# Ordering early output products around a LayerNorm's sums, and holding GpSimd's additions until the keys are written

## The chip, the cores and the metric

The kernel runs on one core of a Trainium2 chip. Five engines work side by side, each through its own queue in order: TensorE (PE in the profile; its weight loads are PEld), VectorE (DVE), ScalarE (ACT), GpSimd (POOL), and SyncE (SP), which only starts transfers. TensorE reads on-chip memory (SBUF) and writes accumulation banks (PSUM); each tile of 128x512 float32 fills one bank. The metric is the device time of one execution in microseconds (us). A difference of less than 0.2% is hardly told from none here.

## The reference

Two layers of an encoder over 512 tokens of width 1024. Each layer has a SwiGLU block, then a mixing block, then another SwiGLU block and a norm. The change lies in the mixing block, of which this is the core (names as in the reference, with what does not matter left out):

```python
p = h @ w_in[l]
attn = mla_group(p[..., :o_kv], ...)      # 8 heads, queries and keys normalised per head
conv = conv_group(p[..., o_cv:], conv_w[l], conv_b[l], conv_ln_g[l], conv_ln_b[l])
x = x + jnp.concatenate([attn, conv], axis=-1) @ w_out[l]

def conv_group(u_raw, conv_w, conv_b, ln_g, ln_b):
    a, g = u_raw[..., :CONV_W], u_raw[..., CONV_W:]
    u = a * jax.nn.sigmoid(g)
    y = causal depthwise convolution of u, 31 taps
    return jax.nn.silu(layer_norm(y + conv_b, ln_g, ln_b))
```

In `mla_group` the keys are `k = rms_norm(k, k_g)` per head, and attention is chunk-causal with a softmax. So the output projection has eight blocks of 128 rows as its input: four from attention, four from the convolution. The four from attention do not depend on the convolution's LayerNorm.

## The kernel before

**Products.** Every float32 product is made of three matmuls (`mm3`, L166 to L168) on operands that were split into a high part and a remainder: high by high, high by remainder, remainder by high. ScalarE makes the high part (`A.copy`, L173 in `split`), VectorE the remainder (L174).

**Who sets the order.** The program is written as if for one queue. A scheduler with a model of time then places the instructions of each engine; an instruction that is placed later in its engine's queue waits for all ahead of it. `tc.issue_after(ins)` forbids the scheduler to place an instruction of the same engine ahead of `ins`; it adds no wait between engines. `tc.high_priority(CHAIN)` lets the scheduler prefer the instructions inside.

**The keys.** `keys()` makes, for each of four token blocks `t`, the keys' scale `sck` on GpSimd (a power, `rsqrt`, L185) and writes the normalised keys `kn` with two VectorE operations (L816 for 64 columns per head, L818 for 32). `turn(h)` transposes them on TensorE (L849). `order["keys"]` is the last of the four `rsqrt` operations. GpSimd's convolution additions (L970) for taps from `PAUSE` = 16 on, or for channel block 2, and the four transfers that GpSimd starts for the output weights (L154), are kept behind `order["keys"]`.

**The convolution.** Of four blocks of 128 channels, VectorE does blocks 0 and 3 tap by tap (L964), ScalarE and GpSimd do block 1 (ScalarE the product `pr`, L968, in four buffers; GpSimd the addition, L970), and TensorE does the early taps of block 2 (L672) with the rest of its taps on ScalarE and GpSimd. These are spread through the attention of the eight heads: scores (L868), maxima on VectorE (L872), exponentials on ScalarE (L876), transposed probabilities (L891), values (L913), division on VectorE (L916).

**The LayerNorm.** The four blocks are summed (`ysum`, L988 to L990), TensorE makes the mean (`pm`, L992), VectorE subtracts it (L994), ScalarE squares (L196, L199) and VectorE adds the squares (L203). Then one chain runs from engine to engine: TensorE sums over channels (`Stats.sums`, L210, four small matmuls), VectorE adds the epsilon (L217), GpSimd takes the power (L185), VectorE lays the result out as a diagonal (L225), TensorE spreads it over all channels (`spread`, L229), VectorE multiplies (L1006), ScalarE applies gain, bias and silu (L1008), and `split` makes the operands of the convolution's four blocks.

**The early products.** While that chain runs, TensorE can do the attention half of the first four output blocks (`WOG` = 4 banks, 48 matmuls). `early_groups` writes them bank by bank, four attention blocks each: the first bank (`E1` = 1) ahead of the chain, three banks behind it in the program, all behind the last score matmul of head 7. Then follow the convolution's 48 matmuls of these banks, and the other four output blocks.

```python
        early_groups(range(E1))
        ...
            r = st.token(CW, conv_bank)
            pr = spread(r, conv_bank, u[1])
        ...
        early_groups(range(E1, WOG))
```

Of the kernel before, what the change touches and what calls it, by code (L numbers as in the profile page):

```python
# [12 lines left out]
ALU = mybir.AluOpType  # L13
# [6 lines left out]
KD = D // P  # L20
NT = S // P
H = 8
DN = 64
DR = 32
DQ = DN + DR
# [25 lines left out]
GLUP = 0  # L51
EARLY = "s"
PRELOAD = 1
E1 = 1
WOG = 4
CHAIN = 400
WAKE = 10
# [20 lines left out]
def encoder_kernel(ctx: ExitStack, tc: tile.TileContext, xT, consts, vecs, rgain, wgu1, wd1, wdq1,  # L78
# [11 lines left out]
    def nm(s):  # L90
        uid[0] += 1
        return f"{s}{uid[0]}"
# [7 lines left out]
    def bank():  # L100
        return psum.tile([P, S], FP, tag="ps", name=nm("ps"))
# [10 lines left out]
    def tiny(tag, w, dt=FP):  # L112
        return small.tile([P, w], dt, tag=tag, name=nm(tag))

    V, A, G, T = nc.vector, nc.scalar, nc.gpsimd, nc.tensor
# [15 lines left out]
    minus_half = cpool.tile([P, H], FP, name="minus_half")  # L131
# [29 lines left out]
        return wpool.tile([P, WC], FR, tag="wl", name=nm("wl"))  # L161

    order = {}

    def mm3(o, lh, ll, rh, rl, first, last, free=False):
        T.matmul(o, lh, rh, start=first, stop=False, skip_group_check=free)  # L166
        T.matmul(o, lh, rl, start=False, stop=False, skip_group_check=free)  # L167
        order["mm"] = T.matmul(o, ll, rh, start=False, stop=last, skip_group_check=free).ins  # L168
        return order["mm"]
# [52 lines left out]
    def spread(r, made=bank, dg=None):  # L222

        dg = tmp() if dg is None else dg
        V.tensor_tensor(dg.rearrange("p (t j) -> p t j", t=NT),  # L225
                        ident[:, None, :].to_broadcast([P, NT, P]),
                        r[:, :, None].to_broadcast([P, NT, P]), ALU.mult)
        ps = made()
        order["spread"] = T.matmul(ps, ones, dg, start=True, stop=True).ins  # L229
        return ps  # L230
# [7 lines left out]
    def group(o, w, rhs, ks, n, ts=slice(0, S)):  # L238

        for k in ks:  # L240
            c = slice(k * P, (k + 1) * P)
            order["product"] = mm3(o, w[0][:, c], w[1][:, c], rhs[k][0][:, ts], rhs[k][1][:, ts], k == 0, k == n - 1)
# [386 lines left out]
    def mix_body(kpool, l, gx, norm, done):  # L629
        u, order = [], {}  # L630
# [53 lines left out]
        kn = kpool.tile([P, NT, H, DQ], FP, tag="kn", name=nm("kn"), bufs=1)  # L684
# [118 lines left out]
        def keys():  # L803
            wk = load_w(wkv[l, 0], WC, "uk")
            for t in range(NT):
                ps = up_kv(wk, t)
                A.copy(kn[:, t, :, 0:DN], ps.rearrange("p (h d) -> p h d", h=H))
                j = tmp()
                A.activation(j, ps, AF.Square)
                V.tensor_reduce(ssk[:, t], j.rearrange("p (h d) -> p h d", h=H), axis=AX.X, op=ALU.add)  # L810
                V.tensor_scalar(ssk[:, t], ssk[:, t], ckc[:, t:t + 1], None, ALU.add)
                sck = small.tile([P, H], FP, tag="sck", name=nm("sck"))
                order["keys"] = rsqrt(sck, ssk[:, t])
                scp = small.tile([P, H], FP, tag="scp", name=nm("scp"))
                V.tensor_scalar(scp, sck, ratio[:, t:t + 1], None, ALU.mult)
                V.tensor_tensor(kn[:, t, :, 0:DN], kn[:, t, :, 0:DN],  # L816
                                sck[:, :, None].to_broadcast([P, H, DN]), ALU.mult)
                V.tensor_tensor(kn[:, t, :, DN:DQ], cke[:, t, None, :].to_broadcast([P, H, DR]),  # L818
                                scp[:, :, None].to_broadcast([P, H, DR]), ALU.mult)


        first = groups([wcv[l, 0], wcv[l, 1]], gx)
# [12 lines left out]
        at = []  # L835
# [3 lines left out]
        heads = [{} for _ in range(H)]  # L839
# [109 lines left out]
        with tc.issue_after(order["keys"]):  # L949
            wo = [load_w(wout[l, m], WC, "sum") for m in range(WOP)]  # L950
        cw, cb = vv(l, "cw"), vv(l, "cb")
        for c, n in enumerate(TAPS):
# [4 lines left out]
            for s in range(n, CK):  # L957
                k = CK - 1 - s
# [6 lines left out]
            for s in range(PT if c == PC else 1, n):  # L965
                k = CK - 1 - s
# [8 lines left out]
                V.tensor_tensor(ys[c][:, n:], ys[c][:, n:], acc[:, n:], ALU.add)  # L975
        early = []

        def early_groups(ms):
            with tc.issue_after(heads[H - 1][EARLY]):
                for m in ms:  # L980
                    early.append(bank())
                    group(early[m], wo[m], at, range(4), KD)

        early_groups(range(E1))
        st = Stats()
        with tc.high_priority(CHAIN):
            ysum = u[1]
            G.tensor_tensor(ysum, ys[0], ys[1], ALU.add)  # L988
            G.tensor_tensor(ysum, ysum, ys[2], ALU.add)
            V.tensor_tensor(ysum, ysum, ys[3], ALU.add)  # L990
            pm = conv_bank()
            T.matmul(pm, onesm, ysum, start=True, stop=True)  # L992
            for c in range(4):
                V.tensor_tensor(ys[c], ys[c], pm, ALU.subtract)  # L994
                st.add(ys[c], eng=V, into=(u[2], u[1], diag.rearrange("p a b -> p (a b)"), u[1])[c])
            r = st.token(CW, conv_bank)
            pr = spread(r, conv_bank, u[1])
        if PRELOAD:
            with behind(heads[H - 1]["exps"]):
                A.activation(tiny("pre", 1), ysum[:, 0:1], AF.Silu)  # L1000
        early_groups(range(E1, WOG))
        lg, lb = vv(l, "lg"), vv(l, "lb")
        cv = []
        for c in range(4):
# [7 lines left out]
        for m0 in range(0, KD, WOG):  # L1012
            ms = range(m0, min(m0 + WOG, KD))
# [272 lines left out]
```

## Time and profile before

| what | us |
|---|---|
| time, median of 3 runs | 1802.54 (1801.73 to 1802.81) |
| the profiled execution's own time | 1799.38 |
| its span, first to last instruction | 1797.6 |
| TensorE busy | 1780.6 |
| VectorE busy | 1501.2 |
| ScalarE busy | 1093.8 |
| GpSimd busy | 384.1 |

The page of the profile gives busy times, the chain that ended last and the costliest groups. Three other views are used below. The view of waits lists for each engine what it sat idle for, in total, how many times, and the longest. The timeline lists instructions with start, duration, engine, line, operation and, in brackets, the idle time ahead of them with what ended it. The view of windows gives for a stretch of time the busy time and, in brackets, the count of instructions of PE, PEld, DVE, ACT and POOL, then TensorE's granted clock (1.00 is full speed), the transfers' share and GB/s. A matmul's duration is longer than its distance to the next one, since matmuls overlap in the pipeline; TensorE's pace is read from starts.

Attention and output projection of layer 0 lie at about 440 to 545 us of the span, those of layer 1 at about 1330 to 1435 us.

### The profile page before, as it was taken

Reading aid. Unit: us, or ns where it says so; the run is one execution under the profiler, and the core shown is the slowest. Engines: PE = TensorE matmul, PEld = TensorE weight load, DVE = VectorE, ACT = ScalarE, POOL = GpSimd, SP = SyncE. Lnnn points to the kernel's source line nnn. Section 1 sums busy time; section 2 is a strip of 40 time slices with the busy share of each in tenths; the row PEclk is TensorE's granted clock in tenths of the full one; section 3 lists DMA queues with packets and bytes.
Section 4 is the critical chain, followed back from the end, with each engine's and each line's share of the span. In section 5 each row is a group of like instructions: output and inputs, shape, how many; then the busy total and the mean of one; then the engine's idle time right before and its main releaser. Section 6 shows DMA issues by size and latency. Waiting matters only on the chain.

```text
span 1797.6 us, 29443 instructions
## 1 busy us (share of the span) xinstructions
PE 1780.6 (99%) x11430; PEld 1579.2 (88%) x11430; DVE 1501.2 (84%) x2309; ACT 1093.8 (61%) x1699; POOL 384.1 (21%) x313
## 2 busy tenths in 40 slices
PE   9999999999999999999999999999999999999998
PEld 7899999888668899999888999998976788999997
DVE  7898988589965989898779989876999568989883
ACT  5665756467853575756645666554777435657564
POOL 1000000258722000000310000002685310000002
PEclk9999999999999999999999999999999999999999
DMA  5657574325203466665426575743260136575742
GB/s 169 168 134 186 130 180 119 109 88 128 61 24 100 125 166 161 153 161 127 125 63 170 127 191 125 193 109 114 77 171 7 35 92 162 138 181 135 182 118 73
DMA packets 71947, 228.28 MB, mean 127 GB/s; under 512 B 8448, under 2 KB 9600, under 8 KB 71808
## 3 DMA queue, kind: packets, MB, share of 16 engines
q1 hardware_dynamic: 55536, 171.87, 30.6%
q0 software_dynamic: 16128, 54.53, 18.0%
q8 instruction: 89, 1.46, 0.3%
q14 instruction: 50, 0.41, 0.1%
q10 hardware_dynamic: 144, 0.00, 0.0%
HBM read 222.19 MB, written 2.10 MB: 125 GB/s over the span
## 4 chain that ended last, share of the span: by engine, by line
PE 89%; DVE 7%; ACT 1%; issue 1%; POOL 1%; DMA 1%; SPq 0%; ACTq 0%; DVEq 0%
PE ps L166 23%; PE ps L167 23%; PE ps L168 23%; PE ps L385 11%; PE ps L386 6%; DVE cv L964 1%; DVE mx L872 1%; PE ps L913 1%; POOL sck L185 1%; DVE r L894 0%; DVE kn L818 0%; PE ps L891 0%; PE ps L210 0%; DVE r L851 0%; PE ps L672 0%
## 5 line engine op out<-in xcount | busy, mean ns | idle before, releaser
L166 PE MATMUL ps<-r,wh 128*128 128x256 f32 (+1 forms) x2556 | 811.6, 321 | 6.8 <-ACT r L173 5.7
L167 PE MATMUL ps<-r,wh 128*128 128x256 f32 (+1 forms) x2556 | 813.5, 319 | 0.1
L168 PE MATMUL ps<-r,wl 128*128 128x256 f32 (+1 forms) x2364 | 755.6, 321 | 0.0
L166 PEld LDWEIGHTS ps<-r,wh 128*128 128x128 f32 x2556 | 483.7, 189 | 53.2 <-ACT r L173 7.3
L167 PEld LDWEIGHTS ps<-r,wh 128*128 128x128 f32 x2556 | 484.9, 190 | 36.7 <-DVE r L174 1.5
L168 PEld LDWEIGHTS ps<-r,wl 128*128 128x128 f32 x2364 | 448.6, 190 | 34.3 <-DVE wl L156 0.2
L385 PE MATMUL ps<-xj,wh 128*128 128x512 f32 x864 | 303.8, 391 | 0.0
L150 ACT CAST wh<-raw 128x1024 fp32r<-128x1024 f32 (+3 forms) x148 | 132.3, 900 | 210.1 <-PE ps L167 131.1
L256 ACT CAST wh<-fr 128x1024 fp32r<-128x1024 f32 (+1 forms) x160 | 157.8, 986 | 104.6 <-DVE fr L422 49.3
L402 POOL DMA_DIRECT2D ls<-in_wgu x72 | 62.5, 868 | 734.7 <-ACT ls L401 502.6
L156 DVE TENSOR_TENSOR wl<-raw,wh 128x1024 fp32r<-128x1024 f32 (+3 forms) x132 | 143.4, 1093 | 91.0 <-ACT wh L150 90.3
L258 DVE TENSOR_TENSOR wl<-fr,wh 128x1024 fp32r<-128x1024 f32 (+1 forms) x160 | 181.8, 1137 | 20.1 <-ACT wh L256 20.1
L385 PEld LDWEIGHTS ps<-xj,wh 128*128 128x128 f32 x864 | 161.4, 188 | 30.1
L386 PE MATMUL ps<-xj,ls 128*128 128x256 f32 x576 | 161.3, 280 | 0.0
L970 POOL TENSOR_TENSOR y<-y,pr 128x495 f32<-128x495 f32 (+29 forms) x90 | 121.7, 1353 | 46.4 <-ACT pr L968 41.0
L256 ACT CAST wh<-raw 128x1024 fp32r<-128x1024 f32 (+1 forms) x100 | 98.1, 981 | 45.1 <-PE ps L167 24.2
L258 DVE TENSOR_TENSOR wl<-raw,wh 128x1024 fp32r<-128x1024 f32 (+1 forms) x100 | 113.3, 1133 | 14.3 <-ACT wh L256 13.8
L386 PEld LDWEIGHTS ps<-xj,ls 128*128 128x128 f32 x576 | 108.3, 188 | 0.0
L401 ACT ACTIVATE ls<-fr 128x1024 fp32r<-128x1024 f32 (+1 forms) x56 | 56.1, 1002 | 75.6 <-PE ps L386 41.5
L203 POOL TENSOR_TENSOR r<-r,t 128x512 f32<-128x512 f32 x45 | 74.2, 1658 | 130.2 <-ACT t L199 129.7
L964 DVE SCALAR_TENSOR_TENSOR cv<-m,vec,cv 128x511 f32<-128x511 f32 (+14 forms) x120 | 87.8, 732 | 3.8 <-ACT cv L960 2.1
L402 POOL DMA_DIRECT2D ls<-in_wdq x32 | 27.6, 863 | 261.7 <-ACT ls L401 261.7
(257 smaller groups left out, 2925.1 us busy)
## 6 DMA issues: line engine op xcount, KB each, us to landing
fr<-in_wgu SPq DMA_DIRECT2D x112, 512.0 KB, 4.3
ls<-in_wgu POOLq DMA_DIRECT2D x72, 512.0 KB, 6.5
raw<-in_wgu SPq DMA_DIRECT2D x62, 512.0 KB, 4.6
fr<-in_wdq SPq DMA_DIRECT2D x48, 384.0 KB, 4.7
ls<-in_wdq POOLq DMA_DIRECT2D x32, 384.0 KB, 4.8
raw<-in_wd SPq DMA_DIRECT2D x32, 384.0 KB, 3.1
raw<-in_wd SPq DMA_DIRECT2D x32, 256.0 KB, 2.8
raw<-in_wcv SPq DMA_DIRECT2D x16, 512.0 KB, 3.5
```

Of the source, the lines that this page charges most:

```text
L150: order["cast"] = A.copy(hi[:, :w], raw[:, :w]).ins
L156: (G if kind in POOLW.split() else V).tensor_tensor(lo[:, :w], raw[:, :w], hi[:, :w].bitcast(FP), ALU.subtract)
L166: T.matmul(o, lh, rh, start=first, stop=False, skip_group_check=free)
L167: T.matmul(o, lh, rl, start=False, stop=False, skip_group_check=free)
L168: order["mm"] = T.matmul(o, ll, rh, start=False, stop=last, skip_group_check=free).ins
L256: A.copy(hi[:, :w], src[:, :w])
L258: order["lo"] = V.tensor_tensor(lo[:, :w], src[:, :w], hi[:, :w].bitcast(FP), ALU.subtract).ins
L385: T.matmul(o, w[0][:, c], both, start=start and k == 0, stop=False, skip_group_check=True)
L386: last = T.matmul(o[:, 0:HS], w[1][:, c], both[:, 0:HS], start=False, stop=k == 3, skip_group_check=True).ins
L402: G.dma_start(out=lo[:, :n], in_=w, accum_op=ALU.add)
L964: V.scalar_tensor_tensor(acc[:, s:], u[c][:, :S - s], tap(k), acc[:, s:], ALU.mult, ALU.add)
L970: order["conv"] = G.tensor_tensor(ys[c][:, s:], ys[c][:, s:], pr[:, s:], ALU.add).ins
```

## The change

Three things change.

- The 48 early matmuls are cut into 16 steps of three, `(m, k)` with `m` the bank and `k` the attention block: first blocks 0 to 2 of bank 0, then of banks 1, 2, 3, then block 3 (the last that attention delivers) of all four banks. Two steps (`EA`) may stand as early as before, four more (up to `EB` = 6) must stand behind the LayerNorm's sums, and the other ten behind the spread.
- `ordered` reads the outer table `order`, in which `Stats.sums` and `spread` leave their matmuls, since the mixing block has a table of its own under that name.
- After the keys, GpSimd does one more operation on one column (`kw`), which reads the last element of `kn`. It must wait for VectorE's last write, and `order["keys"]` is now this operation. So the additions and the four weight transfers on GpSimd stand behind it.

```diff
-E1 = 1
+EA = 2
+EB = 6
...
+    def ordered(name):
+        return order[name]
...
+            order["keys"] = G.tensor_tensor(tiny("kw", 1), kn[:, NT - 1, H - 1, DQ - 1:DQ], minus_half[:, 0:1],
+                                            ALU.mult).ins
...
-        def early_groups(ms):
-            with tc.issue_after(heads[H - 1][EARLY]):
-                for m in ms:
-                    early.append(bank())
-                    group(early[m], wo[m], at, range(4), KD)
-
-        early_groups(range(E1))
+        steps = [(m, k) for m in range(WOG) for k in range(3)] + [(m, 3) for m in range(WOG)]
+
+        def early_steps(a, b, behind_):
+            with tc.issue_after(behind_):
+                for m, k in steps[a:b]:
+                    if k == 0:
+                        early.append(bank())
+                    group(early[m], wo[m], at, (k,), KD)
+
+        early_steps(0, EA, heads[H - 1][EARLY])
...
             r = st.token(CW, conv_bank)
+            sums = ordered("sums")
             pr = spread(r, conv_bank, u[1])
+            spreading = ordered("spread")
...
-        early_groups(range(E1, WOG))
+        early_steps(EA, EB, sums)
+        early_steps(EB, len(steps), spreading)
```

In the changed file every line behind these stands some lines lower: `mm3` is L170 to L172, the values L919, the additions of squares L207, the sums L214, the spread L233, GpSimd's additions L976, its weight transfers L155, the writes of the keys L820 and L822, and `kw` L824.

What stands where is shown below, first of before, then of the change. TensorE's queue in layer 0, at the end of the attention (`ps_5374` holds the last pair of heads, `ps_5619` and `ps_5662` the first two early banks, `cv_5649` the sums), before:

```order
L168 MATMUL ps_5619<-r_5291,wl_5393 128x512
L166 MATMUL ps_5662<-m_5156,wh_5398 128x512
L913 MATMUL ps_5374<-r_5339,m_4774 64x512
...
L913 MATMUL ps_5374<-r_5346,m_4801 64x128
L166 MATMUL ps_5619<-r_5357,wh_5391 128x512
...
L166 MATMUL ps_5688<-m_5156,wh_5412 128x512
L167 MATMUL ps_5688<-m_5157,wh_5412 128x512
L210 MATMUL cv_5649<-ones,m_4633 128x1 x4
L166 MATMUL ps_5619<-r_5385,wh_5391 128x512
...
L168 MATMUL ps_5688<-r_5385,wl_5414 128x512
L229 MATMUL cv_5658<-m_4058,ones 128x512
```

The same place in the change (`ps_5376`, `ps_5621`, `ps_5661` and `cv_5645` are the same buffers):

```order
L172 MATMUL ps_5621<-r_5293,wl_5395 128x512
L919 MATMUL ps_5376<-r_5341,m_4776 64x512
...
L919 MATMUL ps_5376<-r_5348,m_4803 64x128
L214 MATMUL cv_5645<-ones,m_4635 128x1 x4
L170 MATMUL ps_5621<-r_5359,wh_5393 128x512
...
L172 MATMUL ps_5661<-r_5359,wl_5402 128x512
L233 MATMUL cv_5654<-m_4058,ones 128x512
L170 MATMUL ps_5671<-m_5158,wh_5407 128x512
...
L172 MATMUL ps_5681<-r_5387,wl_5416 128x512
```

The sums moved from behind 22 early matmuls that follow the last values to directly behind those values; the spread now has 12 early matmuls between it and the sums, and 30 early matmuls behind it, where it had none.

VectorE's queue at the same place, before (L203 adds the squares, `t_5383` is the last pair of heads divided):

```order
L203 TENSOR_TENSOR m_4633<-m_4633,m_4058 128x512
L203 TENSOR_TENSOR m_4633<-m_4633,m_3846 128x512
L203 TENSOR_TENSOR m_4633<-m_4633,m_4058 128x512
L916 TENSOR_TENSOR t_5383<-ps_5374,t_5372 128x512
L174 TENSOR_TENSOR r_5386<-t_5383,r_5385 128x512
```

And in the change:

```order
L207 TENSOR_TENSOR m_4635<-m_4635,m_4058 128x512
L207 TENSOR_TENSOR m_4635<-m_4635,m_3846 128x512
L922 TENSOR_TENSOR t_5385<-ps_5376,t_5374 128x512
L207 TENSOR_TENSOR m_4635<-m_4635,m_4058 128x512
L178 TENSOR_TENSOR r_5388<-t_5385,r_5387 128x512
```

The third addition of squares, for which the sums wait, moved behind the division, which waits for the last value matmul.

GpSimd's queue behind the keys' scales, before (`y_3848` is channel block 1's result, `pr` a product of ScalarE):

```order
L185 TENSOR_TENSOR sck_4559<-ssk_3863,minus_half 128x8
L154 DMA wl_5393<-in_wout 128x1024
L970 TENSOR_TENSOR y_3848<-y_3848,pr_5496 128x496
L154 DMA wl_5400<-in_wout 128x1024
L970 TENSOR_TENSOR y_3848<-y_3848,pr_5499 128x495
```

And in the change:

```order
L189 TENSOR_TENSOR sck_4559<-ssk_3863,minus_half 128x8
L824 TENSOR_TENSOR kw_4565<-kn_3856,minus_half 128x1
L155 DMA wl_5395<-in_wout 128x1024
L155 DMA wl_5402<-in_wout 128x1024
L976 TENSOR_TENSOR y_3848<-y_3848,pr_5498 128x496
L976 TENSOR_TENSOR y_3848<-y_3848,pr_5501 128x495
```

The operation `kw` stands ahead of all transfers and additions that follow the scales. ScalarE's products of the convolution stand a few places later among the exponentials, and VectorE's taps and maxima change places here and there; SyncE's queue is the same.

## The prediction

> **What bounds the kernel now.** I read the page first, then TensorE's waits, then the two places that they name.
>
> ```profile
> span 1797.6 us, 29443 instructions
> PE 1780.6 (99%) x11430; PEld 1579.2 (88%) x11430; DVE 1501.2 (84%) x2309; ACT 1093.8 (61%) x1699; POOL 384.1 (21%) x313
> PE 89%; DVE 7%; ACT 1%; issue 1%; POOL 1%; DMA 1%; SPq 0%; ACTq 0%; DVEq 0%
> ```
>
> TensorE is busy 99% of the span and carries 89% of the chain that ended last. No matmul is removed, so only its idle time (17.0 us) and slow clock can go. Its waits:
>
> ```profile
> PE ps L166 <- ACT r L173: 5.7, 2, 2.8
> PE ps L849 <- DVE kn L818: 1.1, 2, 0.9
> ```
>
> Once in each layer TensorE waits 2.8 us for the first operand behind the LayerNorm, and once for the keys (0.9 and 0.2). These are the change's two places. Other stretches, by windows:
>
> ```profile
> 460.00:480.00 20.00, 19.96 (x170) 13.53 (x169) 19.71 (x39) 20.00 (x51) 19.06 (x16) 1.00 0.05 18
> 1390.00:1412.00 22.00, 19.16 (x84) 13.23 (x85) 10.57 (x17) 8.46 (x15) 1.03 (x1) 0.98 0.00 0
> 1412.00:1430.00 18.00, 18.00 (x74) 14.30 (x74) 9.68 (x9) 9.46 (x15) 7.69 (x4) 0.93 0.19 56
> ```
>
> In the attention (first row) TensorE, VectorE, ScalarE and GpSimd are all full at once: nothing is to be won there, and a shift can cost. Behind layer 1's wait the granted clock is 0.93.
>
> **The LayerNorm's tail.** TensorE's timeline, layer 0:
>
> ```profile
> 504.67 2.37 PE L913 MATMUL ps<-r,m 128*64 128x512 f32 x14
> 506.96 0.50 PE L166 MATMUL ps<-r,wh 128*128 128x512 f32 x1
> ...
> 512.18 0.95 PE L210 MATMUL cv<-ones,m 128*128 128x1 f32 x8
> 512.99 0.48 PE L166 MATMUL ps<-r,wh 128*128 128x512 f32 x1
> 513.31 0.40 PE L167 MATMUL ps<-r,wh 128*128 128x512 f32 x1
> ...
> 517.25 0.39 PE L168 MATMUL ps<-r,wl 128*128 128x512 f32 x1
> 517.48 1.02 PE L229 MATMUL cv<-m,ones 128*128 128x512 f32 x2
> 521.34 1.20 PE L166 MATMUL ps<-r,wh 128*128 128x512 f32 x4 [2.84 <-ACT r L173]
> ...
> 524.19 1.07 PE L166 MATMUL ps<-r,wh 128*128 128x512 f32 x4
> ```
>
> VectorE's and ScalarE's part:
>
> ```profile
> 504.14 2.27 DVE L203 TENSOR_TENSOR m<-m,m 128x512 f32<-128x512 f32 x3
> 507.07 0.69 DVE L916 TENSOR_TENSOR t<-ps,t 128x512 f32<-128x512 f32 x1 [0.66 <-PE ps L913]
> ...
> 514.47 0.69 DVE L225 TENSOR_TENSOR m<-cst,rtok 128x512 f32<-128x512 f32 x1 [1.14 <-POOL rtok L185]
> 518.54 0.69 DVE L1006 TENSOR_TENSOR m<-m,cv 128x512 f32<-128x512 f32 x1 [3.37 <-PE cv L229]
> ```
>
> ```profile
> 520.68 0.60 ACT L173 CAST r<-m 128x512 fp32r<-128x512 f32 x1
> ```
>
> The squares were added by 506.41, but the sums stood behind 22 early matmuls until 512.18. From the sums' start to the diagonal's end took 2.98 us (to 515.16); then the spread waited for its turn until 517.48; from the spread to the first convolution matmul took 3.86 us, and TensorE had no early matmul left for it.
>
> Now the new order, layer 0. The pace is 0.232 us a matmul (513.31 to 517.25, 17 steps). One early matmul less stands ahead of the last values, which end at 507.04 - 0.23 = 506.81. Here is the new wait: the third addition of squares now stands behind the division L916, which waits for those values. Division from 506.84, addition 0.6 later and 0.69 long: the squares are complete at about 508.15, not 506.41. TensorE reaches the sums at 506.73 and must load their weights first (I take 0.15 to 0.2 that a running queue hides), so it starts at about 508.35: a wait of 1.6 us. The sums take 0.81 (512.18 to 512.99), to 509.2. The diagonal is ready at 508.35 + 2.98 = 511.3. The 12 matmuls between end at 509.2 + 2.8 = 512.0, so the spread waits for nothing, by 0.7 us. First convolution operand: 512.0 + 3.86 = 515.9. TensorE has the spread (about 0.85) and 30 matmuls (7.0) until 519.8. The 2.84 us wait vanishes with 3.9 us to spare; that cover is the 30 early matmuls, and block 3's share of it needs the last division, done at 507.5, and its split, long before. GpSimd's power and ScalarE's silu table move along inside the 2.98 and the 3.86. Saved per layer: 2.84 - 1.6 = 1.25; both layers 2.5. Bounds: 1.0 per layer (the wait at the sums reaches 1.85) to 2.8 (none).
>
> **The clock.** The same matmuls behind the wait, layer 1:
>
> ```profile
> 1410.62 1.80 PE L166 MATMUL ps<-r,wh 128*128 128x512 f32 x4 [2.84 <-ACT r L173]
> 1412.21 0.63 PE L167 MATMUL ps<-r,wh 128*128 128x512 f32 x1
> ...
> 1415.07 1.08 PE L166 MATMUL ps<-r,wh 128*128 128x512 f32 x4
> ```
>
> Between the two groups of four lie 4.45 us here and 2.85 in layer 0 (521.34 to 524.19): after an equal wait layer 1 ran at about half pace for a while, 1.6 us lost. The nearest shorter wait, 0.9 at the keys, has no slow stretch behind it. A wait of 1.6 us lies between; I take no slow stretch, so 1.6 won, bounds 0 (one remains) and -1.6 (both layers get one) downwards; 3.2 upwards, if the timed runs lose the clock in both layers, which one profile can't show.
>
> The Trainium skill, "TensorE: Matmul & The Clock Gate", section "What's actually happening", says that the clock halves after an idle window of about 3.4 us that runs freely, whenever the work comes. By that rule a 2.84 us wait may or may not be punished, as layers 1 and 0 show, and a wait of 1.6 us never is: the sum by it is the same 1.6, with 0 and 3.2 as luck.
>
> **The keys.** VectorE's timeline, layer 0:
>
> ```profile
> 432.86 0.68 DVE L816 TENSOR_TENSOR kn<-kn,sck 128x512 f32<-128x512 f32 x1
> ...
> 435.55 0.76 DVE L818 TENSOR_TENSOR kn<-cke,scp 128x256 f32<-128x256 f32 x2
> ...
> 437.56 2.34 DVE L818 TENSOR_TENSOR kn<-cke,scp 128x256 f32<-128x256 f32 x1
> 439.83 1.94 DVE L815 TENSOR_SCALAR scp<-sck,ratio 128x8 f32<-128x8 f32 x1
> ...
> 442.29 1.46 DVE L818 TENSOR_TENSOR kn<-cke,scp 128x256 f32<-128x256 f32 x1
> ```
>
> GpSimd's at the same time:
>
> ```profile
> 429.30 8.15 POOL L185 TENSOR_TENSOR sck<-ssk,minus_half 128x8 f32<-128x8 f32 x4
> 437.41 0.91 POOL L154 DMA_DIRECT2D wl<-in_wout  x1
> 438.07 1.55 POOL L970 TENSOR_TENSOR y<-y,pr 128x496 f32<-128x496 f32 x1
> ...
> 439.87 4.98 POOL L970 TENSOR_TENSOR y<-y,pr 128x495 f32<-128x495 f32 x3
> ```
>
> A write of 0.38 us (two in 0.76) takes 2.34 and 1.46 as soon as GpSimd's additions run. Held behind `kw`, these are gone: the last block's write ends near 437.56 + 0.4 + 0.15 + 0.6 + 0.4 = 439.1 and not 443.75, ahead of TensorE's need at 442.9. TensorE's wait for the keys goes: 1.1 us in both layers. Nothing is late next there: the value products that follow have their operands. Bounds 0 to 1.1.
>
> What `kw` costs: the nearest row is GpSimd's small product for the rotary tables.
>
> ```profile
> L724 POOL TENSOR_TENSOR tab<-cst,rg x16: 316/323/1303, 14.2 to 426.3; 128x64 f32<-128x64 f32 x16
> ```
>
> So 0.3 us (1.3 if blocked), and behind it wait four weight transfers and 30 additions. They start at about 439.5, 2.1 us later than 437.41. Cover:
>
> ```profile
> 483.18 1.60 POOL L989 TENSOR_TENSOR m<-m,y 128x512 f32<-128x512 f32 x1
> ```
>
> ```profile
> 498.01 0.64 DVE L990 TENSOR_TENSOR m<-m,m 128x512 f32<-128x512 f32 x1
> ```
>
> GpSimd ends its sum at 484.8 and VectorE uses it at 498.0: 13 us of room. The weights are needed by the early products, just ahead of 504.67. Cost on the path: 0. Moves among exponentials, taps and maxima I also take at 0, with 1.0 us a layer either way, since all engines are full there.
>
> **Sum.** 2.5 + 1.6 + 1.1 = 5.2 us. The profiled execution would go from 1799.38 (1797.6 span and 1.8 around it) to 1794.2. It was 3.2 us faster than the median of the runs; taken from 1802.54 the same saving gives 1797.3.
>
> **Rivals.**
> - *More than that.* The timed runs lose the clock in both layers, or the wait at the sums is shorter: up to 1.6 + 1.2 more, about 1794.5. For it: the timed runs are 3.2 us slower than the profiled one. Against: no row says why.
> - *The clock falls at the sums instead.* The 1.6 us wait, now in the middle of the early products, brings a slow stretch of 1.6 us in both layers: 2.5 - 1.6 + 1.1 = 2.0 won, 1800.5, no change by 0.2% (3.6 us). For it: the stretch shows that waits of this size are near the edge. Against: half as long as the wait that was punished only once in two.
> - *The keys' writes stay slow,* because GpSimd's powers block them as its additions do: 4.1 won, 1798.4. Against: L816 at 432.86 took 0.68 while powers ran. The Trainium skill, "SBUF — State Buffer", section "Who interferes with whom", has GpSimd and a two-input VectorE operation exclude each other for the whole instruction, whatever GpSimd computes; by that rule powers would block too, and the row disagrees.
> - *Slower: ScalarE stuck on GpSimd.* ScalarE's queue runs in order, and a convolution product (L968) whose buffer GpSimd has not freed holds up the exponentials behind it.
>
> ```profile
> 449.60 1.28 ACT L968 ACTIVATE pr<-m,vec 128x488 f32<-128x488 f32 x2
> ```
>
> ```profile
> 452.73 10.52 POOL L970 TENSOR_TENSOR y<-y,pr 128x488 f32<-128x488 f32 x8
> ```
>
> The product of 488 is made some 2 us ahead of its addition (made by 450.9, used at 452.73); additions take 1.3 (10.52 over 8), four buffers hold 5.2, so a delay of about 3 us is absorbed. `kw` delays by 2.1. If the keys' last write stayed at 443.75, the delay would be 6.7, and 3.7 us a layer would reach the exponentials and TensorE: 2 x 3.7 - 4.1 = 3.3 lost, 1805.8. It decides from a delay of 3 + 2 = 5 us on. Against: that needs the writes slow with the additions out of the way.
>
> **How the numbers follow.** Forecast 0.52 (alone 1795.5 to 1799.5), more 0.19, clock 0.13, slow keys 0.05, slower 0.11. The forecast and "more" count as faster (1797.3 is 0.29% below, the bound of what can be told is 1798.9), slow keys too, less a few hundredths at the edge: 0.73. Same: clock and that edge, 0.16. Slower 0.11. The range goes from 1793.5 (the "more" case and 1 us of the attention) to 1801.0 (the clock case and half a us); outside are the slower case and the far ends.
>
> **What the profile after would show.** Right: no wait of L170 for ScalarE behind the spread; a new wait of the sums (L214) for VectorE's L207 of 1.4 to 1.8 us a layer; the spread about 3.7 us after the sums with 12 matmuls between; writes of the keys (L822) all near 0.4 us and no wait for them; GpSimd's first addition about 2 us later against the keys; granted clock 1.00 in the tail of layer 1. Wrong: waits of L876 or L891 that grow by more than 1 us a layer, ScalarE's L968 waiting for L976 among the exponentials, or a slow stretch behind the sums.

## The result, and the profile after

The changed kernel takes 1798.23 us (median of 17 runs, 1795.97 to 1800.44) against 1801.73 us of the kernel before on the same chip (17 runs, 1800.12 to 1804.74). The ratio is 0.9981, with a 95% interval of 0.9974 to 0.9989: 3.5 us won, where 5.2 were forecast. That is 0.19%, right at the bound of what a measurement can tell here. The profiled execution took 1796.52 us, 2.9 less than the one before (1799.38).

The page of the changed kernel:

```profile
span 1794.7 us, 29439 instructions
PE 1780.7 (99%) x11430; PEld 1582.0 (88%) x11430; DVE 1481.5 (83%) x2309; ACT 1093.0 (61%) x1699; POOL 381.5 (21%) x315
PE 93%; DVE 4%; ACT 1%; DMA 1%; issue 0%; POOL 0%; SPq 0%; ACTq 0%; DVEq 0%
```

TensorE's busy time is the same to 0.1 us (1780.6 before), so its idle time fell by 3.0 us, from 17.0 to 14.0. A slow clock in one tail had counted as busy time before, and it is gone. Something else must have added busy time in its place; that is followed up below. TensorE's waits:

```profile
PE cv L214 <- DVE m L207: 2.8, 2, 1.4
PE ps L874 <- ACT r L882: 1.0, 2, 0.5
```

The waits for L173 and for the keys' L818, which headed the list before, are gone. The new wait of the sums stands there as forecast, once in each layer, and a score product of the attention waits 0.5 us for ScalarE's exponentials (L882) in both layers; before, that was once in all. In the timeline of TensorE, layer 0 and then two rows of layer 1:

```profile
505.05 2.37 PE L919 MATMUL ps<-r,m 128*64 128x512 f32 x14
508.79 1.05 PE L214 MATMUL cv<-ones,m 128*128 128x1 f32 x8 [1.38 <-DVE m L207]
...
512.58 1.02 PE L233 MATMUL cv<-m,ones 128*128 128x512 f32 x2
...
520.32 1.07 PE L170 MATMUL ps<-r,wh 128*128 128x512 f32 x4
...
1397.44 1.05 PE L214 MATMUL cv<-ones,m 128*128 128x1 f32 x8 [1.38 <-DVE m L207]
...
1408.98 1.07 PE L170 MATMUL ps<-r,wh 128*128 128x512 f32 x4
```

VectorE in layer 0:

```profile
507.45 0.69 DVE L922 TENSOR_TENSOR t<-ps,t 128x512 f32<-128x512 f32 x1 [1.24 <-PE ps L919]
508.06 0.68 DVE L207 TENSOR_TENSOR m<-m,m 128x512 f32<-128x512 f32 x1
```

The last values end at 507.42 (505.05 + 2.37). The division L922 stands ahead of the third addition of squares L207, and the sums start only after both. From the sums to the spread it is 3.79 us, and the first convolution products (four L170) come with no wait in front of them.

Both tails in one view, windows of 30 us, first the kernel before and then the changed one (length, busy time and instructions of TensorE, its weight loads, VectorE, ScalarE, GpSimd; then the granted clock):

```profile
500.00:530.00 30.00, 27.16 (x130) 19.80 (x127) 13.62 (x23) 12.23 (x20) 1.43 (x2) 1.00 0.00 1
1390.00:1420.00 30.00, 27.16 (x114) 19.69 (x115) 12.46 (x20) 10.00 (x17) 1.03 (x1) 0.94 0.00 1
```

```profile
500.00:530.00 30.00, 28.62 (x140) 21.27 (x138) 16.74 (x25) 14.29 (x22) 4.40 (x3) 1.00 0.00 1
1390.00:1420.00 30.00, 28.62 (x129) 21.36 (x130) 16.98 (x25) 14.30 (x23) 5.73 (x3) 1.00 0.04 11
```

TensorE's idle time falls from 2.84 to 1.38 us in each layer, and in layer 1 the clock goes from 0.94 to 1.00, that is 1.8 us of 30.

The keys, VectorE and then GpSimd, layer 0:

```profile
438.78 0.41 DVE L822 TENSOR_TENSOR kn<-cke,scp 128x256 f32<-128x256 f32 x1
...
439.85 0.41 DVE L822 TENSOR_TENSOR kn<-cke,scp 128x256 f32<-128x256 f32 x1
```

```profile
440.34 0.19 POOL L824 TENSOR_TENSOR kw<-kn,minus_half 128x1 f32<-128x1 f32 x1 [1.67 <-DVE kn L822]
440.56 1.82 POOL L155 DMA_DIRECT2D wl<-in_wout  x2
```

The writes that had taken 2.34 and 1.46 us take 0.41, `kw` takes 0.19, and the last write is done ahead of TensorE's need.

**Where the gain went.** Both kernels issue 11430 matmuls, and outside attention and tail in one order. So the start of each can be set against the start of the same one before. In the attention the changed kernel wins 0.65 and 0.67 us (not where it was forecast; see "The keys alone"), in the tails 1.73 and 3.51: 6.6 us. But it loses in the four feed-forward stretches, whose code is the same line by line. The rows of the feed-forward's joined products in the four stretches (minimum, median and maximum of a matmul in ns, first and last start), before and then after:

```profile
L385 PE MATMUL ps<-xj,wh x216: 387/389/400, 77.7 to 311.7; 128*128 128x512 f32 x108
L385 PE MATMUL ps<-xj,wh x216: 387/390/400, 624.6 to 858.6; 128*128 128x512 f32 x108
L385 PE MATMUL ps<-xj,wh x216: 387/390/400, 966.9 to 1201.0; 128*128 128x512 f32 x108
L385 PE MATMUL ps<-xj,wh x216: 387/390/400, 1515.7 to 1749.7; 128*128 128x512 f32 x108
```

```profile
L389 PE MATMUL ps<-xj,wh x216: 389/393/423, 77.9 to 312.9; 128*128 128x512 f32 x108
L389 PE MATMUL ps<-xj,wh x216: 389/393/423, 623.3 to 858.2; 128*128 128x512 f32 x108
L389 PE MATMUL ps<-xj,wh x216: 389/393/423, 966.8 to 1201.6; 128*128 128x512 f32 x108
L389 PE MATMUL ps<-xj,wh x216: 389/393/423, 1512.0 to 1746.9; 128*128 128x512 f32 x108
```

From the first to the last it was 234.0 us and is now 234.8 to 235.0, in every stretch: 3.6 us together. No wait explains it. Most steps from the start of a matmul that streams an `xj` or `xs` tile to the start of the next one are 1 to 4 ns longer, all along the stretch (one kind, `xs` with `wh` twice in a row, is 2.4 ns shorter). What the change gives the feed-forward is one thing only: the new tile `kw` takes 64 bytes of each partition (two buffers of 32), and every tile allocated behind it stands 64 bytes further on: `fr` (169696 to 169760), `xj` (186080 to 186144), `xs` and `ls`. The ring, the weights' tiles and the temporaries stay where they were.

### The profile page after: what moved, and what is told of

Read it like the earlier page. It is cut to its first block, busy times and chain, and to the rows that moved or that the text cites. A ratio compares the mean times of both kernels' runs of the same rounds, so it can differ in the third digit from the quotient of the medians.

```text
span 1794.7 us, 29439 instructions
## 1 busy us (share of the span) xinstructions
PE 1780.7 (99%) x11430; PEld 1582.0 (88%) x11430; DVE 1481.5 (83%) x2309; ACT 1093.0 (61%) x1699; POOL 381.5 (21%) x315
## 3 DMA queue, kind: packets, MB, share of 16 engines
q8 instruction: 89, 1.46, 0.3%
## 4 chain that ended last, share of the span: by engine, by line
PE 93%; DVE 4%; ACT 1%; DMA 1%; issue 0%; POOL 0%; SPq 0%; ACTq 0%; DVEq 0%
PE ps L170 24%; PE ps L172 23%; PE ps L171 23%; PE ps L389 11%; PE ps L390 6%; PE ps L919 1%; PE ps L874 1%; PE ps L897 1%; DVE cv L970 1%; DVE mx L878 1%; PE ps L912 0%; PE ps L676 0%; PE ps L214 0%; DVE wl L262 0%; DMA r<-m 0%
## 5 line engine op out<-in xcount | busy, mean ns | idle before, releaser
L170 PE MATMUL ps<-r,wh 128*128 128x256 f32 (+1 forms) x2556 | 810.3, 320 | 2.7 <-ACT wh L1114 1.1
L172 PE MATMUL ps<-r,wl 128*128 128x256 f32 (+1 forms) x2364 | 755.4, 321 | 0.0
L170 PEld LDWEIGHTS ps<-r,wh 128*128 128x128 f32 x2556 | 485.1, 190 | 47.5 <-ACT wh L151 3.7
L172 PEld LDWEIGHTS ps<-r,wl 128*128 128x128 f32 x2364 | 449.1, 190 | 34.1 <-DVE wl L157 0.4
L976 POOL TENSOR_TENSOR y<-y,pr 128x495 f32<-128x495 f32 (+29 forms) x90 | 120.4, 1341 | 45.9 <-ACT pr L974 40.6
L207 POOL TENSOR_TENSOR r<-r,t 128x512 f32<-128x512 f32 x45 | 73.7, 1648 | 136.8 <-ACT t L203 136.5
```

The lines of the kernel that those rows point to most:

```text
L976: order["conv"] = G.tensor_tensor(ys[c][:, s:], ys[c][:, s:], pr[:, s:], ALU.add).ins
```

## The experiments

The theory is that this shift of addresses costs the feed-forward 3.6 us ("address"). The rival is that the loss comes from the reordering or from the profiled execution ("order"). The first four runs take the change apart along both lines.

**kw without a tile.** The changed kernel, but `kw`'s result goes to a column that nothing reads any more:

```diff
-            order["keys"] = G.tensor_tensor(tiny("kw", 1), kn[:, NT - 1, H - 1, DQ - 1:DQ], minus_half[:, 0:1],
+            order["keys"] = G.tensor_tensor(first_gain[:, 0:1], kn[:, NT - 1, H - 1, DQ - 1:DQ], minus_half[:, 0:1],
```

> The changed kernel, but the small product kw writes into the first column of first_gain, which nothing reads any more, so that its 64 bytes in the pool of small tiles are gone and every tile behind them stands where it stood before the change. Order and instructions are those of the changed kernel. Theory 'address' (the feed-forward's matmuls run some 2 to 4 ns slower each because their tiles moved by 64 bytes): the four feed-forward stretches get the pace of the kernel before back, 3.6 us in all; the time is 6 to 7 us below the kernel before, about 1795. Theory 'order' (the feed-forward is slower after the reordering for another reason, or by the execution that was profiled): the feed-forward stays about 3.6 us slower than before, and the time is that of the changed kernel, 3.5 us below the kernel before, about 1798.

Measured: 1794.59 us (5 runs), ratio 0.9964 (0.9950 to 0.9977) against 1801.3 of the kernel before, 6.7 us less. Its second feed-forward stretch:

```profile
L389 PE MATMUL ps<-xj,wh x216: 387/390/400, 622.1 to 856.2; 128*128 128x512 f32 x108
```

The duration is that of before (387/390/400), and first to last is 234.1. All four stretches together differ from the kernel before by 0.1 us, while attention and tails win 6.6 as in the changed kernel. "Address" holds, "order" falls.

**The 64 bytes alone.** The kernel before and an unused tile:

```diff
+    V.memset(small.tile([P, 1], FP, tag="pad", name=nm("pad"), bufs=2), 0.0)
     minus_half = cpool.tile([P, H], FP, name="minus_half")
```

> The kernel before, with nothing but an unused tile of 64 bytes in the pool of small tiles (one write of one column at the start), so that the feed-forward's and the keys' tiles stand where the changed kernel has them. Theory 'address': about 3.6 us slower than the kernel before, all of it in the four feed-forward stretches, the matmuls that read xj and xs some 2 to 4 ns slower each. Theory 'order': the time of the kernel before within 0.5 us.

Measured: 1803.83 us (11 runs), ratio 1.0016 (1.0007 to 1.0025), 2.5 us slower; the interval (1.3 to 4.5) holds the 3.6 expected. The same stretch:

```profile
L386 PE MATMUL ps<-xj,wh x216: 389/393/423, 625.3 to 860.2; 128*128 128x512 f32 x108
```

Minimum, median and maximum are those of the changed kernel to the nanosecond, and first to last is 234.9. An unused tile alone makes the loss.

**Early steps alone.** The changed kernel without the line of `kw`, so that the keys' part is that of before:

```diff
-            order["keys"] = G.tensor_tensor(tiny("kw", 1), kn[:, NT - 1, H - 1, DQ - 1:DQ], minus_half[:, 0:1],
-                                            ALU.mult).ins
```

> The early products in steps around the sums and the spread, without kw: the keys' part is that of the kernel before, and so are all addresses. By the prediction's terms, the tail (1.25 a layer forecast, 2.84 - 1.38 = 1.46 in the changed kernel's profile) and the clock (1.6): 4.1 to 4.6 us below the kernel before under 'address', with the feed-forward at the pace of before. Under 'order', if the reordering itself slows the feed-forward, 4.5 - 3.6, that is 1 us below at most.

Measured: 1795.85 us (6 runs), ratio 0.9969 (0.9958 to 0.9981), 5.5 us less; 4.1 to 4.6 were expected, which the interval (3.4 to 7.6) holds. The feed-forward has its old pace (0.0 us over the four stretches). Layer 1's attention wins 0.47 us here, though nothing of the keys is changed; that is taken up with the next run. Its profile also shows something that I had given little weight, in layer 0 behind the new wait:

```profile
504.89 2.37 PE L917 MATMUL ps<-r,m 128*64 128x512 f32 x14
508.64 1.20 PE L214 MATMUL cv<-ones,m 128*128 128x1 f32 x8 [1.38 <-DVE m L207]
509.70 0.77 PE L170 MATMUL ps<-r,wh 128*128 128x512 f32 x1
510.27 0.63 PE L171 MATMUL ps<-r,wh 128*128 128x512 f32 x1
...
512.83 0.40 PE L171 MATMUL ps<-r,wh 128*128 128x512 f32 x1
```

```profile
500.00:530.00 30.00, 28.62 (x132) 21.14 (x131) 15.18 (x24) 13.96 (x22) 2.98 (x2) 0.94 0.00 1
```

The wait is 1.38 us as in the changed kernel, where the clock stayed at 1.00. Here it fell to 0.94 over the window: the matmuls of 0.63 instead of 0.40 us are a stretch at half clock. So a slow stretch can follow the new wait too.

**The keys alone.** The kernel before, with `kw` written to `first_gain` and GpSimd's additions behind it:

```diff
+            order["keys"] = G.tensor_tensor(first_gain[:, 0:1], kn[:, NT - 1, H - 1, DQ - 1:DQ], minus_half[:, 0:1],
+                                            ALU.mult).ins
```

> The keys' part alone: kw is there and GpSimd's additions wait for it, but it writes into first_gain, so no address moves; the early products are those of the kernel before. The prediction's term is 1.1 us below the kernel before for both layers; the two profiles show 0.65 a layer in the attention, so 1.1 to 1.3 below. Should kw's delay of GpSimd cost something that the early products hide, it comes out at 0 or slower.

Measured: 1800.18 us (11 runs), ratio 0.9995 (0.9986 to 1.0003). A median 1.1 us lower, as expected, but the interval takes in no change, so the time alone does not settle it. In the trace the keys' wait is gone from the list, and from ahead of the keys to the end of the attention TensorE wins 0.67 us over the kernel before, in both layers.

These are not the same microseconds. Setting start against start through the attention, TensorE is 1.08 us ahead right behind the keys in layer 0 and 0.42 in layer 1. At about 476 and 1369 us of the kernel before nothing of that is left (0.01 in both), and that holds for all five profiles with the keys' change. ScalarE has no room in between, before and in the changed kernel (of the whole 32 us it is busy 31.97 in both):

```profile
445.00:477.00 32.00, 31.84 (x246) 20.02 (x247) 31.09 (x58) 31.97 (x76) 29.72 (x25) 1.00 0.46 112
```

```profile
445.00:477.00 32.00, 31.35 (x240) 20.10 (x240) 29.53 (x55) 31.97 (x75) 29.45 (x25) 1.00 0.53 125
```

The 0.67 us arise behind that place. VectorE, which has hardly any idle time there, makes a remainder of two inputs while GpSimd adds, first before and then in the changed kernel:

```profile
480.10 3.01 POOL L970 TENSOR_TENSOR y<-y,pr 128x483 f32<-128x483 f32 x2
482.01 1.64 DVE L174 TENSOR_TENSOR m<-t,m 128x512 fp32r<-128x512 f32 x1
```

```profile
480.53 4.46 POOL L976 TENSOR_TENSOR y<-y,pr 128x485 f32<-128x485 f32 x3
483.23 0.68 DVE L178 TENSOR_TENSOR m<-t,m 128x512 fp32r<-128x512 f32 x1
```

Before, the remainder starts in the middle of an addition, which runs until 483.11, and takes 1.64 us. In the changed kernel it starts within 0.12 us of an addition's start and takes 0.68, and it is the addition that takes 1.9 us instead of 1.2. In the 13 profiles and two layers there are 26 such places. In the ten with the keys' change the remainder takes 0.67 or 0.68 us and TensorE gains 0.65 to 0.67; in two others (layer 1 of the early steps alone and of the kernel with 32 unused bytes, below) it takes 1.03 and 1.05 and TensorE gains 0.47 and 0.50; in the remaining 14 it takes 1.64 or 1.65 and nothing is gained (0.03 at most). So the attention's gain goes with the place of that one operation among GpSimd's additions, which the keys' change happened to shift. No run shifts it alone.

This execution had bad luck with the clock, in layer 0:

```profile
521.79 2.07 PE L166 MATMUL ps<-r,wh 128*128 128x512 f32 x4 [2.84 <-ACT r L173]
523.67 0.63 PE L167 MATMUL ps<-r,wh 128*128 128x512 f32 x1
...
527.08 1.43 PE L166 MATMUL ps<-r,wh 128*128 128x512 f32 x4
```

```profile
500.00:530.00 30.00, 27.16 (x120) 19.45 (x118) 13.27 (x22) 11.02 (x18) 1.03 (x1) 0.89 0.00 1
1390.00:1420.00 30.00, 27.16 (x134) 19.38 (x131) 14.94 (x26) 11.07 (x19) 1.03 (x1) 0.94 0.00 1
```

Behind the 2.84 us wait the half clock lasted twice as long in layer 0 (0.89 of the window), and it came in layer 1 as well. This layout of the tail loses the clock in either layer, not in the second alone.

**More steps ahead of the sums.** If the 1.38 us wait is time to be had, more early products ahead of the sums should fill it. In the kernel without `kw`'s tile:

```diff
-EA = 2
-EB = 6
+EA = 4
+EB = 8
```

> The changed kernel with kw written into first_gain (no address moves) and two steps more ahead of the sums and of the spread each (EA 4, EB 8): six matmuls more before the sums, one of them ahead of the last values, 12 between sums and spread as now, 24 instead of 30 behind the spread. Theory 'the wait at the sums is time to be had': the last values end 0.23 us later, so the squares too; five early matmuls (1.16 us) fill what was a wait of 1.38 us, of which 0.3 to 0.4 stays. 1.0 us a layer, and no slow clock behind the sums: 2 us and somewhat more below the kernel without kw's tile (1794.6), about 1792.5. Rival 'the cover behind the spread becomes too short': the spread to the first convolution operand takes 3.9 us, 24 matmuls and the spread itself cover 6.4; only if that is not enough does a wait for ScalarE come back, and the time stays at 1794.6 or above.

Measured: 1790.84 us (5 runs, 1789.93 to 1791.01), ratio 0.9940 (0.9928 to 0.9953) against 1801.83. That is 3.75 us below the kernel without the tile (4.3 when each is set against its own runs of the kernel before), more than the 2 forecast. VectorE and TensorE in layer 0, and the windows:

```profile
504.13 2.27 DVE L207 TENSOR_TENSOR m<-m,m 128x512 f32<-128x512 f32 x3
507.06 0.69 DVE L922 TENSOR_TENSOR t<-ps,t 128x512 f32<-128x512 f32 x1 [0.66 <-PE ps L919]
```

```profile
507.99 0.40 PE L172 MATMUL ps<-m,wl 128*128 128x512 f32 x1
508.22 0.95 PE L214 MATMUL cv<-ones,m 128*128 128x1 f32 x8
```

```profile
500.00:530.00 30.00, 30.00 (x144) 22.54 (x141) 17.29 (x26) 15.87 (x26) 5.09 (x3) 1.00 0.02 4
1390.00:1420.00 30.00, 30.00 (x139) 23.70 (x138) 17.46 (x23) 16.10 (x25) 9.09 (x5) 1.00 0.11 35
```

With the new numbers the order put all three additions of squares ahead of the division again, which I had not foreseen. So no rest of the wait is left, and TensorE is busy for the whole 30 us in both layers; set start against start, the two tails win 1.43 and 1.44 us over the kernel without the tile. The rival, a cover behind the spread that gets too short, falls: no wait of L170 for ScalarE is there. The five timed runs lie within 1.1 us of each other, where the 17 runs of the kernel before lie within 4.6 and the 17 of the changed kernel within 4.5. A stretch at half clock costs 1.6 to 1.8 us, so this spread would be two or three of them. The granted clock of the timed runs fits that. Profiles without a slow stretch have a mean of 0.999 or 1.000 over the execution. So have all ten timed runs of this version and of the one with 128 unused bytes below. Of the changed kernel's 17 runs ten have 0.997 or 0.998, and they take 2.1 us longer in the mean (1799.4 against 1797.3); of the 70 runs of the kernel before beside the experiments 54 have 0.998 or less.

**Other shifts.** Three kernels with 32, 128 and 96 unused bytes in the kernel before, made like the 64 (one buffer of 32 bytes, two of 64, three of 32):

> The kernel before with 32 bytes ahead of the feed-forward's and the keys' tiles: they then start on a multiple of 64 and 128 bytes, where they start 96 bytes behind such a multiple before and 32 behind it in the changed kernel. Theory 'the place within 128 bytes sets the pace': this is another place, so another pace, faster or slower than both by up to 0.8 us in each of the four feed-forward stretches. Theory 'the distance between the operands' tiles sets it': no forecast of the sign. If the pace is that of the kernel before, the start within 64 bytes plays no part.

> The kernel before with 128 bytes ahead of the same tiles: every tile stands at the same place within 128 bytes as in the kernel before. Theory 'the place within 128 bytes': the pace of the kernel before in all four feed-forward stretches, and its time, within 0.5 us. Theory 'distance': the pace differs again, by 0.8 us or more a stretch (1.6 if it grows with the shift).

> The kernel before with 96 bytes ahead of the same tiles: they start 64 bytes behind a multiple of 128. Theory 'the place within 128 bytes': a fourth place; together with the shifts of 0, 32, 64 and 128 it shows whether the pace goes by the start within 64 bytes (then equal to the shift of 32) or within 128. Theory 'it grows with the shift': slower than the shift of 64, by some 4.5 us against the kernel before.

The column "stretch" is first to last start of the joined products in the second feed-forward stretch, from rows like those above; the last three columns are how much longer than before it is, in ns, from the start of one matmul to that of the next (operands: streamed tile, weights), worked out from the starts in the traces of that stretch. Two more kernels, told of below, stand in the same table; the times of before beside which they ran were 1801.2 to 1801.8:

```
unused bytes           time us  ratio (95%)              stretch   xj,wh to xj,ls   xj,wh to xj,wl   xs,wh to xs,wl
none (before)          1801.3   -                        234.0     0 (228.8)        0 (230.6)        0 (115.9)
32                     1800.87  0.9995 (0.9986, 1.0004)  234.0     0.0              0.7              1.6
64                     1803.83  1.0016 (1.0007, 1.0025)  234.9     2.2              3.4              4.1
96                     1802.11  1.0000 (0.9991, 1.0009)  234.5     2.3              0.9              3.5
128                    1799.95  0.9989 (0.9980, 0.9998)  233.8     2.2              0.1              0.8
64 from xj on          1803.29  1.0010 (1.0001, 1.0019)  234.9     2.3              3.5              3.8
64 from xs on          1802.84  1.0014 (1.0005, 1.0023)  234.8     4.1              0.0              4.3
```

The table leaves out the steps back to `xj,wh`. From `xj,ls` that step (118.1 ns before) is 1.1 to 1.5 ns longer with 64 bytes ahead of `xj`, but 3.1 shorter with 32 and 2.3 shorter with 128, so that the stretches of these two come out even or better.

The loss does not grow with the shift: 128 bytes are better than none, by 0.2 us in the stretch and 1.9 us in the median. That is also less than the 0.8 us a stretch which the theory of the distance had. Nor does the loss go by the place within 128 bytes, which the shift of 128 leaves the same: its steps differ from those of before, and its median is 1.9 us lower (0.4 to 3.6 by the interval) where that theory allowed 0.5. The start within 64 bytes does not decide either, since 32 and 96 share it and differ by 0.5 us.

**Which tiles.** The kernel before with 64 unused bytes inside the feed-forward's pool, once between `fr` and `xj`, once between `xj` and `xs`:

```diff
+                if not spaced:
+                    spaced.append(fpool.tile([P, 16], FP, tag="pad", name=nm("pad"), bufs=1))
+                    V.memset(spaced[0], 0.0)
                 both = fpool.tile([P, 2, S], FR, tag="xj", name=nm("xj"), bufs=WIDE)
```

> The kernel before with 64 unused bytes between the feed-forward's fr tiles and its xj tiles: xj, xs, ls, e and u stand where the changed kernel has them, fr and the keys' tiles where the kernel before has them. Theory 'the operands that TensorE reads' (xj, xs, ls): the whole loss of the 64 bytes, 0.8 us a stretch, 3.2 in all. Theory 'fr' (where the weights land by DMA and which VectorE and ScalarE read): nothing, the pace of the kernel before.

> The kernel before with 64 unused bytes between the xj tiles and the xs tiles: only xs, ls, e and u stand where the changed kernel has them. Theory 'xj alone': no loss. Theory 'xs and ls': 3.2 us in all. The matmuls that read xj with wh took the larger part of the loss (some 210 a stretch, 2.3 to 3.4 ns each, against 32 of xs with wl at 4.2), so that I expect most of the loss to be gone here: 0 to 1 us slower than the kernel before.

The first has the whole loss, so `fr` plays no part and the tiles from `xj` on do. The second went against my expectation: with `xj` back in its place the loss stays, 234.8 against 234.0 in the stretch. The last columns of the table show where it sits now. While TensorE streams `xj` with the weights `wh`, it loads the next weights. If those are in `ls` (moved), the step takes 4.1 ns longer; if they are in `wl` (not moved), nothing. With `xj` moved as well, the step to `wl` pays 3.5, and the step to `ls` 2.3 instead of 4.1. So it is neither tile alone: these steps go by the tile that is streamed and the tile whose weights are loaded meanwhile, together. By which rule of the two addresses, these runs don't say, nor do they show by what mechanism.

The Trainium skill, "SBUF — State Buffer", section "Who interferes with whom", gives TensorE one read port for the streamed operand and an independent one for the weight load, and says that it never waits for anyone. Taken at its word, that leaves no reason for a shift to cost anything; 0.8 to 0.9 us in the second stretch of four kernels with a 64 byte shift speak against it, and the measurement decides.

**Both together.** The version with more steps ahead, and 128 unused bytes:

> The version with more early steps ahead of the sums (EA 4, EB 8, kw in first_gain), with 128 unused bytes ahead of the feed-forward's tiles. By the profile of the shift of 128 alone the feed-forward's steady pace gains 0.24 to 0.35 us in each of its four stretches: 1.2 us below the same version without the shift (1790.8), about 1789.6. If the shifts' effect does not carry over to this version, or is noise of the executions, 1790.8.

Measured: 1788.76 us (5 runs, 1788.62 to 1789.27), ratio 0.9931 (0.9918 to 0.9945) against 1801.22, 2.1 us below the version without the shift. Set against the same matmuls of the version without the shift, the steady pace wins 0.21, 0.26, 0.35 and 0.34 us in the four stretches, 1.2 us as forecast. This is the fastest version found, 12.5 us below the kernel before.

## Why the prediction was right, and where it was wrong

The direction came out as forecast and the time lies inside the range, but errors of opposite sign stand behind that. By the two traces tails and attention won 6.6 us against 5.2 in the sum, and a part that the sum priced at nothing lost 3.6. The attention's 1.3 of these 6.6 came about in another way than forecast; that the sum's 1.1 is near it is luck.

- *The failed step: "What `kw` costs".* The working priced the operation (0.3; measured 0.19) and the delay of GpSimd's queue (2.1; measured 1.9, the first transfer at 440.56 against 437.41 in a trace that runs 1.2 us late there), found both covered, and wrote "Cost on the path: 0". Both are covered. But the tile that the operation writes was not looked at. Its 64 bytes cost 3.6 us in stretches that the change does not touch. No rival had this either.
- *The keys, a second failed step: "Nothing is late next there".* TensorE's wait went, and with it 1.08 and 0.42 us (1.1 for both in the sum). But ScalarE had next to no idle time in the attention that follows (busy 31.97 of 32 us), and TensorE had lost all of the gain again within some 35 us. In layer 0, 0.5 us of that is one wait of a score product for ScalarE's exponentials, which the kernel before has in layer 1 alone. The 0.65 and 0.67 us that remain come from VectorE's remainder that no longer falls into an addition of GpSimd. "The keys' writes stay slow" falls all the same: the writes take 0.41 us everywhere, some of them while GpSimd's powers run.
- *The LayerNorm's tail.* The mechanism holds at each step: the 2.84 us wait is gone, the new one stands at the sums behind the division, the spread comes 3.79 us after the sums (3.7 forecast), and the first convolution operand is ready with 3.9 us to spare (ScalarE writes it by 516.39, TensorE uses it at 520.32). The term was too small: the new wait is 1.38 us and not 1.6. VectorE's two operations take what I had for them (from 507.45 to 508.74), but the sums start 0.05 us behind them (at 508.79) where I had 0.2 for their weights, and I had counted the wait from 0.08 us ahead of the values' end. In layer 0, which ran at full clock in both executions, the tail wins 1.73 us instead of 1.25; 1.46 of it is waiting, the other 0.27 is spread over small gaps that I have not put down to anything.
- *The clock.* In the two profiles 1.8 us came back in layer 1, near the 1.6 of the sum, but these are one execution each. Seven profiles beside that of before keep the 2.84 us wait in both layers; with it that makes 16 such waits, and half clock followed 8 of them (one twice as long), in either layer. So a kernel with this tail can lose the clock in both layers of one execution (the keys alone did), which was the first rival's reason. Behind the 1.38 us wait half clock followed 1 of 6 in the profiles (two each in the changed kernel, the one without the tile and the one with the early steps alone), and where no wait is left at the sums, 0 of 4. The timed runs count against "I take no slow stretch" more strongly: ten of the changed kernel's 17 have a granted clock of 0.998 or less, as none of the ten runs without a wait at the sums has. So the second rival's reason came true in part. By the mean granted clock (0.9978 over 70 runs of the kernel before, 0.9984 over 17 of the changed one) the clock's part is about 1.1 us of 1800, an estimate, and not 1.6. Where in the timed runs the clock fell is not on record.
- *The idle window.* The Trainium skill, "TensorE: Matmul & The Clock Gate", section "What's actually happening", puts the bound at an idle window of about 3.4 us, and I had concluded that a wait of 1.6 us is never punished. The early steps alone show half clock behind 1.38 us, so the conclusion does not hold. TensorE had next to no work there for 2.4 us, since the sums behind the wait stream one column each (from 507.26, the values' end, to 509.70). That little work counts, and not the wait alone, would fit; no run here takes the two apart.
- *"Slower: ScalarE stuck on GpSimd"* falls: the delay stayed at 1.9 us, and the attention came out 0.67 us a layer shorter with `kw` alone.
- *The cover.* GpSimd's sum and VectorE's use of it:

```profile
486.35 1.28 POOL L998 TENSOR_TENSOR m<-m,y 128x512 f32<-128x512 f32 x1
```

```profile
498.27 0.69 DVE L999 TENSOR_TENSOR m<-m,m 128x512 f32<-128x512 f32 x1
```

GpSimd ends 2.8 us later than before (487.6) and 10.6 us of its 13 us of room remain.

## What to carry over

An instruction that is added for its wait has a result, and the result has an address: where a pool packs tiles one behind the other, a new small tile moves all that come later, so compare the tiles' addresses as well as the instructions, and write a throw-away result into memory that is already there. When a change moves the time less than its parts should, set the start of each matmul against the same one before: a loss that grows evenly over code that is unchanged is pace, not a wait. The same comparison shows whether a gain lasts: a wait that vanishes ahead of a stretch in which another engine is full can be gone again at its end. And a short wait followed by tiny matmuls cost the clock in some executions, so the version to look for is the one without the wait; its five runs also scattered less.

## What was not expected of the hardware

- A shift of 64 bytes of the tiles that TensorE reads lengthened most steps between their matmuls by 1 to 4 ns (of 116 to 231), and a feed-forward stretch of 234 us by 0.8 to 0.9, without any wait in the profile. A shift of 128 bytes shortened the stretch by 0.2. The steps that were taken apart go by the streamed tile and the weights that are loaded meanwhile together; the rule is open.
- Half clock after a wait of 1.38 us (0.63 instead of 0.40 us a matmul of 512 columns, for some 3 us, 1.6 us lost), once in six in the profiles, and after 8 of 16 waits of 2.84 us.
- One VectorE operation with two inputs, of 128x512, took 1.64 us when it started in the middle of an addition of GpSimd and 0.68 when it started together with one. In the 26 such places of 13 profiles TensorE's gain in the attention goes with it: 0.65 to 0.67 us in a layer where it took 0.68, none where it took 1.64.
